# Instance normalisation over rows: giving each partition 512 consecutive rows, 8 MB from its neighbour, in place of four rows, 64 KB from its neighbour

## The chip, the cores and the metric

One core of a Trainium2 chip, with its 16 DMA engines and nothing else running. The metric is device time in microseconds (us), the median of several executions; lower is better. Executions are compared within one state (those used here are of the fast state, unless a sentence says otherwise). The kernel before has two close levels: most of its executions took 4962 to 4970 us, some 5004 to 5012. Differences of 1% are not read from a few runs here.

## The reference

```python
x = np.random.randn(256, 256, 4096).astype(np.float32)     # 65,536 rows of 16 KiB, 1.07 GB
mean = np.mean(x, axis=2, keepdims=True)
var = np.var(x, axis=2, keepdims=True)
return (x - mean) / np.sqrt(var + 1e-5)
```

Every row is normalised by itself, so it doesn't matter for the result which partition handles which row, as long as the row is written back to its place. One warning on "correct": with such an input each row already has a mean near 0 and a variance near 1, and a plain copy of x passes the comparison. The comparison shows that rows land in their places; it is weak on the arithmetic, which the change leaves alone.

## The kernel before

A tile is 128 partitions x 4 rows; 128 tiles make up the tensor. Three buffers of 64 KiB per partition take turns.

```python
x_t = x_flat.rearrange("(t p k) d -> t p k d", p=P, k=K)       # P = 128, K = 4
out_t = out_flat.rearrange("(t p k) d -> t p k d", p=P, k=K)
X = [pool.tile([P, K, d], fp32, name=f"x{s}") for s in range(BUFS)]   # BUFS = 3
```

So tile t is one contiguous piece of 8 MiB, and partition p has 64 KiB of it, right behind those of partition p - 1. One queue (SyncE's) issues all the transfers; a store and the next load alternate in it:

```python
def store(s, t):
    take(S, done[s], K)                  # the four rows are normalised
    S.dma_start(out=rows_of(out_t, t), in_=X[s][:, :, :]).then_inc(stored[s], 16)

def load(s, t, wait=True):
    if wait:
        take(S, stored[s], 16)           # the buffer's last store has landed
    S.dma_start(out=X[s][:, :, :], in_=rows_of(x_t, t)).then_inc(loaded[s], 16)

# ... first tiles cut
with S.Fori(0, rounds) as i:
    for t in range(L0, L0 + BUFS):
        store(t % BUFS, (t, BUFS, rounds, i))
        load((t + 2) % BUFS, (t + 2, BUFS, rounds, i))
# ... last tiles cut
```

VectorE sums each row and later scales three of the four; ScalarE squares and sums each row and scales the fourth. Neither is touched.

## Time and profile before

| | before |
|---|---|
| median of 2 runs | 4963.81 us |
| VectorE, ScalarE busy | 68%, 51% |
| the 16 DMA engines busy | 100% |
| bytes moved per time | 433 GB/s |
| VectorE's wait for loads | 1452.4 us, 126 times |

The DMA engines are busy for the whole span (100%), and the arithmetic waits 11.5 us in each tile for them. The lines that carry this stand in the prediction.

### The profile page before, as it was taken

What the parts mean: (1) busy time and instruction counts of PE and PEld (TensorE: products, weight loads), DVE (VectorE), ACT (ScalarE), POOL (GpSimd) and SP (SyncE); (2) the same over time, 40 slices, a digit from 0 to 9 for tenths busy, and PEclk for the clock granted to TensorE, in tenths of its full rate; (3) what the DMA queues carried; (4) which work ended last, traced back from release to release, by engine and by line L of the source; (5) the groups of instructions that cost most, each with busy time, mean ns of one, the idle gap of its engine ahead of it and who ended that gap; (6) DMA issues with size and microseconds to landing.
All of it is one profiled execution on the core that took longest, in us unless ns stands there. A gap on an engine that the chain in (4) does not pass through costs nothing.

```text
span 4960.3 us, 6348 instructions
## 1 busy us (share of the span) xinstructions
DVE 3390.1 (68%) x2439; ACT 2505.6 (51%) x1416; POOL 0.2 (0%) x4
## 2 busy tenths in 40 slices
DVE  6766666776677766777667776677666776677766
ACT  5555544555445544555445554455544555455545
POOL 0000000000000000000000000000000000000000
DMA  9999999999999999999999999999999999999999
GB/s 423 431 435 430 431 434 433 433 436 433 433 436 432 434 436 432 435 435 433 437 432 434 436 432 434 436 432 433 437 432 434 435 433 435 435 432 438 432 433 406
DMA packets 37299, 2147.52 MB, mean 433 GB/s; under 512 B 4144, under 2 KB 4144, under 8 KB 4144
## 3 DMA queue, kind: packets, MB, share of 16 engines
q1 hardware_dynamic: 37296, 2147.50, 100.0%
q14 instruction: 3, 0.02, 0.0%
HBM read 1073.74 MB, written 1073.74 MB: 433 GB/s over the span
## 4 chain that ended last, share of the span: by engine, by line
DMA 71%; DVE 19%; ACT 7%; another core or an unknown queue 1%; issue 1%; SPq 0%; ACTq 0%; DVEq 0%
DMA x<-in_x_dram 40%; DMA out_dram<-x 31%; DVE part L89 17%; ACT junk L132 3%; ACT x L140 3%; DVE nsum L91 1%; DVE x L110 1%; DVE nmean L93 1%; ACTq L182 0%; ACT std L137 0%; DVE nbias L102 0%; SPq L159 0%; SPq L154 0%; DVE rstd L100 0%
## 5 line engine op out<-in xcount | busy, mean ns | idle before, releaser
L89 DVE TENSOR_REDUCE part<-x 128x64 f32<-128x4096 f32 x512 | 2258.6, 4411 | 1452.4 <-DMA x<-in_x_dram 1452.4
L132 ACT ACTIVATE junk<-x,nmean 128x4096 f32<-128x4096 f32 x512 | 1883.0, 3678 | 2417.0 <-DVE nmean L93 2417.0
L110 DVE TENSOR_SCALAR x<-x,rstd,nbias 128x4096 f32<-128x4096 f32 x382 | 910.2, 2411 | 37.6 <-DVE nbias L102 16.4
L140 ACT ACTIVATE x<-x,nbias,rstd 128x4096 f32<-128x4096 f32 x130 | 492.2, 3786 | 0.0
L91 DVE TENSOR_REDUCE nsum<-part 128x1 f32<-128x64 f32 x512 | 112.4, 220 | 17.7
L132 ACT ACTIVATION_READ_ACCUMULATOR junk<-x,nmean 128x1 f32 x512 | 95.5, 186 | 0.0
L93 DVE TENSOR_SCALAR nmean<-nsum 128x1 f32<-128x1 f32 x512 | 78.5, 153 | 17.5
L100 DVE RECIPROCAL rstd<-std 128x1 f32<-128x1 f32 (+1 forms) x260 | 41.7, 160 | 17.2 <-ACT std L137 16.5
L102 DVE TENSOR_TENSOR nbias<-nmean,rstd 128x1 f32<-128x1 f32 (+1 forms) x260 | 41.6, 160 | 8.9
L137 ACT ACTIVATE std<-ss,eps_tile 128x1 f32<-128x1 f32 x130 | 38.3, 295 | 15.1
L124 ACT ACTIVATE std<-ss,eps_tile 128x3 f32<-128x3 f32 (+1 forms) x130 | 38.5, 296 | 4.2
L132 ACT ACT_TABLE_LOAD x1 | 1.3, 1283 | 1.2 <-DVE eps_tile L211 1.2
L124 ACT ACT_TABLE_LOAD x1 | 1.3, 1283 | 0.0
L211 DVE MEMSET eps_tile<- 128x1 f32 x1 | 0.1, 59 | 1.0 <-SPq L181 1.0
L248 POOL MEMSET const-uint8-127<- 128x1 uint8 x1 | 0.1, 102 | 0.0
L248 POOL MEMSET const-bfloat16-1.0<- 128x1 bf16 x1 | 0.1, 101 | 0.0
L248 POOL MEMSET const-float32-0.0<- 128x1 f32 x1 | 0.1, 98 | 0.2 <-issue 0.2
L248 POOL MEMSET const-float32-1.0<- 128x1 f32 x1 | 0.1, 98 | 0.0
## 6 DMA issues: line engine op xcount, KB each, us to landing
out_dram<-x SPq DMA_DIRECT2D x4, 4096.0 KB, 18.8
x<-in_x_dram SPq DMA_DIRECT2D x2, 4096.0 KB, 16.7
x<-in_x_dram SPq DMA_DIRECT2D x127, 49.2
out_dram<-x SPq DMA_DIRECT2D x126, 30.5
```

Source lines behind the costliest of these rows:

```text
L89: mine(V.tensor_reduce(out=part[s][:, r, :], in_=row, axis=AX.X, op=ALU.add))
L91: mine(V.tensor_reduce(out=nsum[s][:, c], in_=part[s][:, r, :], axis=AX.X, op=ALU.add, negate=True))
L93: V.tensor_scalar_mul(out=nmean[s][:, c], in0=nsum[s][:, c], scalar1=1.0 / d).then_inc(means, 1)
L100: mine(V.reciprocal(out=rstd[s][:, c], in_=std[s][:, c]))
L102: mine(V.tensor_mul(out=nbias[s][:, c], in0=nmean[s][:, c], in1=rstd[s][:, c]))
L110: V.tensor_scalar(out=x[:, r, :], in0=x[:, r, :], scalar1=rstd[s][:, c], scalar2=nbias[s][:, c], op0=ALU.mult, op1=ALU.add,).then_inc(dn, 1)
L124: A.activation(out=std[s][:, r0:last], in_=ss[s][:, r0:last], func=AF.Sqrt, bias=eps_tile, scale=1.0 / d).then_inc(stds, 1)
L132: A.activation(out=junk, in_=x[:, r, :], func=AF.Square, bias=nmean[s][:, c], scale=1.0, accum_out=ss[s][:, c]).then_inc(own_a, 1)
L137: A.activation(out=std[s][:, c], in_=ss[s][:, c], func=AF.Sqrt, bias=eps_tile, scale=1.0 / d).then_inc(stds, 1)
L140: A.activation(out=x[:, last - 1, :], in_=x[:, last - 1, :], func=AF.Identity, bias=nbias[s][:, c], scale=rstd[s][:, c]).then_inc(dn, 1)
L211: V.memset(eps_tile, eps).then_inc(ready, 1)
L248: nc = _bacc.Bacc("TRN2", target_bir_lowering=False, num_devices=1)
```

## The change

Its intent is to give each partition one long stretch of the tensor, 512 consecutive rows, and to walk through it four rows at a time.

```diff
-    x_t = x_flat.rearrange("(t p k) d -> t p k d", p=P, k=K)
-    out_t = out_flat.rearrange("(t p k) d -> t p k d", p=P, k=K)
+    x_t = x_flat.rearrange("(p t k) d -> t p k d", p=P, k=K)
+    out_t = out_flat.rearrange("(p t k) d -> t p k d", p=P, k=K)
```

A partition still takes 64 contiguous KiB of a tile, but the next partition's lie 512 x 16 KiB = 8 MiB further on. "Pitch" is used below for this distance from partition to partition: 64 KiB before, 8 MiB after.

## The prediction

> **What bounds the kernel now.** I read the views in this order: the page's busy shares and DMA rows, the chain of waits, the waits by engine, one tile in the timeline, and the time from issue to landing.
>
> ```profile
> DVE 3390.1 (68%) x2439; ACT 2505.6 (51%) x1416; POOL 0.2 (0%) x4
> ...
> DMA packets 37299, 2147.52 MB, mean 433 GB/s; under 512 B 4144, under 2 KB 4144, under 8 KB 4144
> ...
> q1 hardware_dynamic: 37296, 2147.50, 100.0%
> ...
> DMA 71%; DVE 19%; ACT 7%; another core or an unknown queue 1%; issue 1%; SPq 0%; ACTq 0%; DVEq 0%
> ```
>
> VectorE is busy for 68% of the span and ScalarE for 51%, but the 16 DMA engines are busy for 100% of it. The kernel reads 1073.74 MB and writes as much; 2147.5 MB at 433 GB/s take 4960 us, which is the whole span. The small packets are not data: 259 transfers with 16 semaphore writes each are the 4144 counted under 512 bytes. What remains is data in large pieces. The trace's packet records hold 32,384 packets of 65,536 bytes (one partition's four rows of 16 KiB), the rest in the halved first and last tiles. Their median duration is 2.418 us and their 95th percentile 2.419 us, so an engine moves 65,536 / 2.418 = 27.1 GB/s, and 16 of them 433.7 GB/s, whether the packet reads HBM or writes it.
>
> The chain calls 19% VectorE and 7% ScalarE, which looks as if faster arithmetic would pay. The waits say otherwise:
>
> ```profile
> DVE part L89 <- DMA x<-in_x_dram: 1452.4, 126, 12.2
> ```
>
> VectorE waits for data 126 times, 1452.4 / 126 = 11.5 us a time. One tile in the timeline:
>
> ```profile
> 2009.89 0.34 SPq L154 DMA_DIRECT2D out_dram<-x  x1
> 2010.47 0.35 SPq L159 DMA_DIRECT2D x<-in_x_dram  x1
> 2021.13 4.42 DVE L89 TENSOR_REDUCE part<-x 128x64 f32<-128x4096 f32 x1 [11.49 <-DMA x<-in_x_dram]
> ...
> 2048.46 0.34 SPq L154 DMA_DIRECT2D out_dram<-x  x1
> 2049.04 0.35 SPq L159 DMA_DIRECT2D x<-in_x_dram  x1
> 2059.77 4.42 DVE L89 TENSOR_REDUCE part<-x 128x64 f32<-128x4096 f32 x1 [11.50 <-DMA x<-in_x_dram]
> ```
>
> A tile lands at 2021.13, the next at 2059.77: the period is 38.64 us. From landing to store is 2048.46 - 2021.13 = 27.33 us of arithmetic, and 38.64 - 27.33 = 11.3 us are slack. A tile is 8.39 MB in and 8.39 MB out, which at 434 GB/s is 2 x 19.33 = 38.66 us, the period itself. In each period the one queue holds a store of tile t-1, then the load of tile t+1, so stretches of pure writing and pure reading of some 19 us alternate.
>
> ```profile
> x<-in_x_dram SPq DMA_DIRECT2D x127, 49.2
> out_dram<-x SPq DMA_DIRECT2D x126, 30.5
> ```
>
> These fit the same picture: a store is issued with 11.3 us of the earlier load still ahead and takes 19.3, in all 30.6 (seen: 30.5); the load behind it takes 19.3 more, 49.9 (seen: 49.2).
>
> [...]
>
> [...] The kernel before, with a pitch of 64 KiB, moves 433 / 2 = 217 GB/s per direction[...]. It can't show the slow case.
>
> [...]
>
> **The change part by part.**
>
> 1. Instructions. The order on VectorE, ScalarE, SyncE and the rest is the same as before, row for row (190, 91 and 50 rows). Each partition still takes four adjacent rows of a tile, 65,536 contiguous bytes, so I expect the same 37,296 packets of the same sizes, nothing removed and nothing added. The arithmetic keeps its 27.33 us a tile. Load and store use the same mapping, so each row returns to its place and the result is right.
>
> 2. Addresses. The start of partition p moves from p x 65,536 bytes to p x 512 x 16,384 = p x 8,388,608 bytes: exactly 8 MiB, a power of two, plus 65,536 times the tile's number. In one transfer all 128 packets agree in their address modulo 8 MiB; all that tells the 16 streams apart there is how far each has come in its 64 KiB.
>
> 3. What that costs. [...] A transfer of 8.39 MB takes 40.2 us instead of 19.33, and the period becomes 80.4 us.
>
> 4. What of it is hidden: nothing. The DMA queue already sets the period and its slack is zero. The slack is on the arithmetic's side, 11.3 us a tile, and grows to 80.4 - 27.3 = 53.1.
>
> 5. Sum. 128 x (80.4 - 38.66) = 5,343 us more than 4,964, or 10,307 us. [...] I take 10,300. The ends, where arithmetic isn't overlapped, are some 20 us in either kernel and change nothing.
>
> **The rivals.**
>
> A. It costs little or nothing (about 4,960 us). For it: the order of instructions and the packets stay the same[...]. The packet records show starts scattered over the 2.4 us of a packet, not in step: some 0.15 us apart, which is about 4 KiB of progress. [...]
>
> B. A part of it, say a factor of 1.2 to 1.8 (6,000 to 9,000 us). For it: with 64 KiB in a run the streams of one transfer cover a four times wider window of addresses[...], and the load and the store in flight lie two tiles, 128 KiB, apart in two tensors. If what they share is coarse[...], a wider window means more places to spread over. I can't size it from anything in the profile before.
>
> C. Worse[...] (up to 20,000 us). [...] Here the queue alternates: for 19 us only reads, then only writes. [...] Against it: when engines drift apart at the limit, some will be on the store while others are on the load[...].
>
> D. A new wait takes over. With three buffers, a load of t+2 needs the store of t-1 to have landed, and that store is two places ahead of it on the same queue. As the transfers slow down, every tile of arithmetic has more time, so no engine becomes the bound; I rule this out.
>
> E. It gets faster. [...] One in a hundred.
>
> **The range and the chances.** [...] half of my weight is on a factor of 1.8 to 2.3, or 8,900 to 11,400 us. B has a quarter, A a tenth, C and other ways of being worse 15%. The middle of these is [...] 10,300 us. The range that cuts about a tenth at each side is 6,000 to 13,000 us; it gives up A at one side and the full form of C at the other. Slower by over 2%: 0.90; within 2%: 0.09; faster: 0.01.
>
> **What would show it.** If it is right, the profile after has 37,296 packets again, DMA engines busy all the time, and a mean near 208 GB/s in each of the 40 slices; packets of 64 KiB at about 5.0 us and widely scattered instead of all at 2.418; every group of VectorE and ScalarE with its old mean (4411, 3678, 2411 ns); VectorE's wait for data at 53.1 us a tile, 6,700 us in all; and a store landing 53.1 + 40.2 = 93 us after its issue, a load 133 us. Step 1 is wrong if the number or sizes of packets change, for then the change is one of descriptors and not of addresses. Step 3 is wrong in size if packets take 3 to 4 us (B) or near 10 us (C), and wrong altogether if they keep 2.4 (A). If reads and writes differ, for instance writes slow and reads not, then [...] my single factor is a mean of them. Step 4 is wrong if the period exceeds the packets' time, with the DMA engines idle.

## More of the kernel before

One more view is wanted for later, the rate in 40 equal slices of the span; it is level from the second slice to the last but one:

```profile
GB/s 423 431 435 430 431 434 433 433 436 433 433 436 432 434 436 432 435 435 433 437 432 434 436 432 434 436 432 433 437 432 434 435 433 435 435 432 438 432 433 406
```

## The result, and the profile after

The changed kernel took 7134.01 us (two runs, 7132.27 and 7135.74), with a ratio of 1.437 to the kernel before (95% interval 1.431 to 1.443). Ratios here are the mean time of one kernel's fast runs over that of the other's fast runs in the same rounds, so not quite the ratio of the medians that are quoted. It is slower, as forecast, and inside the range of 6,000 to 13,000 us, but the forecast was 10,300: the kernel lost 2170 us where 5,336 were predicted. The size was wrong.

The page of the changed kernel, with the engines' busy time, the rate by slices, the packets, the shares of the chain, two of the costliest groups, and the times from issue to landing:

```profile
DVE 3390.6 (48%) x2439; ACT 2505.6 (35%) x1416; POOL 0.2 (0%) x4
...
GB/s 247 260 275 305 304 306 305 310 296 302 309 309 305 302 301 297 304 306 313 302 301 301 312 310 302 297 305 310 297 299 286 308 304 308 303 303 309 309 299 317
DMA packets 37299, 2147.52 MB, mean 301 GB/s; under 512 B 4144, under 2 KB 4144, under 8 KB 4144
...
q1 hardware_dynamic: 37296, 2147.50, 97.9%
...
another core or an unknown queue 52%; DVE 45%; issue 2%; ACT 0%; DMA 0%; DVEq 0%; ACTq 0%; SPq 0%
...
L89 DVE TENSOR_REDUCE part<-x 128x64 f32<-128x4096 f32 x512 | 2258.7, 4412 | 3612.3 <-DMA x<-in_x_dram 3612.3
...
L110 DVE TENSOR_SCALAR x<-x,rstd,nbias 128x4096 f32<-128x4096 f32 x382 | 910.3, 2411 | 37.7 <-DVE nbias L102 17.1
...
x<-in_x_dram SPq DMA_DIRECT2D x127, 81.0
out_dram<-x SPq DMA_DIRECT2D x126, 54.3
```

The number of packets is the same to the last one, and so are the engines' busy times (3390.6 us against 3390.1) and the mean of each instruction. All that differs is how long the DMA engines need: 301 GB/s in place of 433, still 97.9% busy. The chain of waits is a trap here: where it said DMA before it says "another core or an unknown queue" for 52%. The kernel has one core, and the view of waits and the timeline name the same stretches, ahead of VectorE's first sum in a tile, as a wait for the load:

```profile
DVE part L89 <- DMA x<-in_x_dram: 3612.3, 127, 44.0
```

```profile
3018.97 4.42 DVE L89 TENSOR_REDUCE part<-x 128x64 f32<-128x4096 f32 x1 [26.56 <-DMA x<-in_x_dram]
...
3046.40 0.34 SPq L154 DMA_DIRECT2D out_dram<-x  x1
3046.98 0.35 SPq L159 DMA_DIRECT2D x<-in_x_dram  x1
3072.74 4.42 DVE L89 TENSOR_REDUCE part<-x 128x64 f32<-128x4096 f32 x1 [26.61 <-DMA x<-in_x_dram]
```

From landing to store is 3046.40 - 3018.97 = 27.43 us, the same arithmetic as before; this tile's period is 53.77 us in place of 38.64, and VectorE waits 26.6 us in it in place of 11.5. Over all tiles the wait is 3612.3 / 127 = 28.4 us. The wait grew by 3612.3 - 1452.4 = 2159.9 us and the span by 7133.6 - 4960.3 = 2173.3: nearly the whole loss is in the wait for transfers.

The trace's packet records say in what form. Duration in ns of the packets of 65,536 bytes, 32,384 in each kernel:

```
kernel    mean   10%   25%   50%   75%   90%   99%   within 1% of the fastest
before    2420  2418  2418  2418  2418  2418  2432   99%
after     3403  2418  2831  3209  3779  4451  6441   13%
```

Packets were nearly all alike, at 2418 ns (99% within 1%); now one in eight (13%) still takes no longer and the rest are held up by different amounts. The mean grew by 3403 / 2420 = 1.406, and the engines are busy 97.9% and not 100%; 1.406 / 0.979 = 1.436 is the measured ratio to within 0.1%.

The trace holds one more thing, which bears on all that follows: the times of the 16 semaphore writes that end each transfer, taken here as one from each engine. In the changed kernel the first and the last engine finished 1.7 us apart in the first of the 40 slices (median of its transfers), 3.6 in the second, 18.4 in the third and 37.6 in the fourth, and some 30 from then on, as long as a whole transfer takes. The rate in these four slices is 247, 260, 275 and 305 GB/s. So the engines start in step and drift apart, and the rate rises as they do. That is a coincidence in time; no run set the drift by itself.

### The profile page after: what moved, and what is told of

Read it like the earlier page. It is cut to its first block, busy times and chain, and to the rows that moved or that the text cites.

```text
span 7133.6 us, 6348 instructions
## 1 busy us (share of the span) xinstructions
DVE 3390.6 (48%) x2439; ACT 2505.6 (35%) x1416; POOL 0.2 (0%) x4
## 3 DMA queue, kind: packets, MB, share of 16 engines
q1 hardware_dynamic: 37296, 2147.50, 97.9%
HBM read 1073.74 MB, written 1073.74 MB: 301 GB/s over the span
## 4 chain that ended last, share of the span: by engine, by line
another core or an unknown queue 52%; DVE 45%; issue 2%; ACT 0%; DMA 0%; DVEq 0%; ACTq 0%; SPq 0%
DVE part L89 31%; DVE x L110 10%; DVE nsum L91 2%; DVE nmean L93 1%; DVE nbias L102 1%; DVE rstd L100 0%; DMA x<-in_x_dram 0%; ACT junk L132 0%; DVEq L68 0%; ACTq L182 0%; DVEq L105 0%; DVEq L214 0%; ACT std L137 0%; ACT L124 0%
## 5 line engine op out<-in xcount | busy, mean ns | idle before, releaser
L89 DVE TENSOR_REDUCE part<-x 128x64 f32<-128x4096 f32 x512 | 2258.7, 4412 | 3612.3 <-DMA x<-in_x_dram 3612.3
## 6 DMA issues: line engine op xcount, KB each, us to landing
out_dram<-x SPq DMA_DIRECT2D x126, 54.3
```

The source lines that it names most:

```text
L89: mine(V.tensor_reduce(out=part[s][:, r, :], in_=row, axis=AX.X, op=ALU.add))
```

## The experiments

Eighteen kernels ran. The questions were: is it the equality of the addresses or the distance; does it hit reads, writes or both; why is the loss 44% and not the 108% that the prediction put on a tile's period (80.4 us in place of 38.66, the author's estimate, which nothing in the profile before showed); and what do copies without the arithmetic lose. The theory for the third, called W, is this: what counts is how wide a window of addresses modulo a large power of two the streams in flight cover. In the changed kernel the 128 packets of a transfer all cover the same 64 KiB modulo 8 MiB. The main rivals are that each start of a packet at a far address has its cost (P), and that reads and writes at once make the difference.

**One direction alone.** First only the loads, then only the stores, use the new mapping. Rows then land in wrong places.

```diff
# first run: before, with
+    x_t = x_flat.rearrange("(p t k) d -> t p k d", p=P, k=K)
# second run: before, with
+    out_t = out_flat.rearrange("(p t k) d -> t p k d", p=P, k=K)
```

> Only the loads use the 8 MiB mapping; the stores keep 64 KiB, so rows land in the wrong place and the result is wrong on purpose. The change cost 7134 - 4964 = 2170 us in both directions. Theory 1 (each direction pays for itself, alike): about half, 4964 + 1085 = 6050 us, with half of the large packets still at 2.418 us. Theory 2 (reads and writes at far addresses get in each other's way): less than a third of it, under 5690 us. Theory 3 (only reads are hurt): near 7130 us.

> Only the stores use the 8 MiB mapping; wrong result on purpose. Theory 1: about 6050 us, and together with the run that moves only the loads the two extra times add up to 2170 us. Theory 2: both extras together clearly under 2170 us. Theory 3 (only reads are hurt): 4964 us here; if only writes are hurt, near 7130 us.

Measured: loads alone 5707.13 us (ratio 1.143), stores alone 6092.67 us (1.220). Against 4964 us these are 743 and 1129 us, together 1872 of the 2170, and far stores cost half as much again as far loads. (The kernel before ran at both of its levels in these rounds; by the ratios, 0.143 and 0.220 of 0.437 leave 0.074, some 370 us, in place of the 298.) The page of each, the rate by slices, the loads' run first:

```profile
GB/s 314 341 350 359 360 367 373 376 380 380 380 380 383 385 381 380 386 389 377 381 387 384 379 380 385 387 379 383 389 381 381 380 390 384 380 384 385 385 377 377
```

```profile
GB/s 318 300 319 343 359 363 349 355 360 362 353 355 356 359 355 349 362 354 364 351 355 358 363 351 355 353 365 354 359 356 360 355 352 359 358 357 351 360 354 342
```

In the first, 66% of the large packets stayed within 1% of the fastest, which would fit half of them being stores at the old addresses. In the second only 37% did, although half are loads at the old addresses: at least a quarter of these loads were held up too, so a far direction also slows the near one, and the 743 and 1129 us are costs to the kernel, not to one direction's own packets. Theory 1 gives the larger part of the loss, with unequal halves; theory 3 falls; of theory 2 there remain the 298 us or so that appear only when both directions are far, and the kernel with reversed stores, below, takes that up.

**Distance or equality.** The same far packets, with a pitch of 511 rows in place of 512.

```diff
-    x_t = x_flat.rearrange("(p t k) d -> t p k d", p=P, k=K)
+    x_t = bass.AP(x_flat.tensor, 0, [[4*d, ntiles], [511*d, P], [d, K], [1, d]])   # out_t alike
```

> The mapping of the change, but with 511 rows in place of 512 from partition to partition: 8 MiB less 16 KiB. Packets are as far apart as before and as long; some rows are done twice and the last 128 not at all, so the result is wrong on purpose. If distance itself costs[...], 7130 us as with 512. If the equality of the addresses modulo a large power of two costs, the time returns to 4964 us within 2%. Something between would say that 16 KiB steps undo only some of the collisions.

Measured: 4990.65 us, ratio 1.0006. All of the loss is gone (interval 0.993 to 1.008), with packets that lie 8 MiB less 16 KiB apart. The page has the rate of the kernel before:

```profile
GB/s 422 433 435 431 435 433 433 436 432 436 434 433 437 432 434 436 432 437 433 433 437 432 435 435 432 437 433 433 436 433 436 434 433 436 433 433 436 432 430 398
```

Being 8 MiB less 16 KiB apart costs nothing here (1.0006); lying at equal addresses modulo 8 MiB does (1.437). What in the memory such addresses share, no trace here shows.

**Shorter runs.** The changed kernel with each transfer cut into four, then into two, and the first cut on the kernel before as a control.

```diff
-        S.dma_start(out=rows_of(out_t, t), in_=X[s][:, :, :]).then_inc(stored[s], 16)
+        for j in range(4):                                     # or 2
+            q = slice(j * K // 4, (j + 1) * K // 4)
+            S.dma_start(out=rows_of(out_t, t)[:, q, :], in_=X[s][:, q, :]).then_inc(stored[s], 16)
# loads alike; the waits for a whole tile go from 16 to 16 * 4
```

> The changed kernel, with each load and store of 64 KiB per partition cut into four transfers of 16 KiB per partition[...], one after the other in the queue. Theory W (a run of 64 KiB lets the streams spread[...]): near [...] 10300 us, packets of 16 KiB at about 1.26 us in place of 0.6. Rival (length of the run does not matter[...]): about 7130 us plus what more packets cost, at most a few per cent.

> Control: the kernel before (64 KiB between partitions) with the same cut into four transfers of 16 KiB per partition. If the 9325 us of the cut far kernel came from the more numerous packets and semaphores, much of it shows here (say over 5500 us). If it came from the addresses, this is 4964 us within 2%.

> The changed kernel with each transfer cut in two, 32 KiB per partition. Whatever the cause of the difference between 64 KiB (ratio 1.437) and 16 KiB (1.868), this should lie between: about 1.6, 7950 us. If it is at either end, there is a step between two sizes and not a slope.

Measured: cut in four 9325.17 us (ratio 1.868), in two 7698.96 us (1.549), the control 5035.49 us (1.012). The first lies between the two times expected, nearer to W's. The control matters: at near addresses four times the packets and semaphores cost 1%, so the rest of the 1.868 is put down to the addresses, 1.868 / 1.012 = 1.85; a cost of each transfer that arises at far addresses alone is not excluded. A shorter run makes it worse, in a slope and not a step (1.437 with 64 KiB, 1.549 with 32, 1.868 with 16). The packets and rates of the cut far kernel and of its control, in this order:

```profile
DMA packets 146596, 2147.58 MB, mean 230 GB/s; under 512 B 16288, under 2 KB 16288, under 8 KB 16288
```

```profile
DMA packets 146597, 2147.58 MB, mean 427 GB/s; under 512 B 16289, under 2 KB 16289, under 8 KB 16289
```

**Packet or window.** The cut changes two things at once: packets become 16 KiB, and the streams of a transfer cover only 16 KiB. This kernel changes only the first. A gap of 64 bytes after each row of the tile on the chip keeps rows from being joined into one packet, while a partition's four rows still follow one another.

```diff
-    X = [pool.tile([P, K, d], fp32, name=f"x{s}") for s in range(BUFS)]
+    X = [pool.tile([P, K, d + 16], fp32, name=f"x{s}")[:, :, :d] for s in range(BUFS)]
```

> The changed kernel with 64 bytes of unused space after each row of 16 KiB in the tiles on the chip: a packet can then hold only one row, 16 KiB, [...] the streams of a transfer still cover 64 KiB. Theory W (what counts is how wide a window of addresses modulo 8 MiB the streams in flight cover): as the changed kernel, about 7130 us, although packets are 16 KiB. Rival P (each start of a packet at a far address costs): as the cut kernel, about 9300 us. Check: packets of 16,384 bytes, 129,000 of them.

Measured: 7099.18 us, ratio 1.428; the trace has 131,072 packets of 16,384 bytes. The page of this kernel:

```profile
DMA packets 135219, 2147.52 MB, mean 303 GB/s; under 512 B 4144, under 2 KB 4144, under 8 KB 4144
```

Packets of 16 KiB cost nothing more here (1.428 against 1.437) as long as the window stays at 64 KiB. P falls, and W stands so far.

**A wider window.** The pitch is 8 MiB less 1 KiB, then 8 MiB less 256 bytes, which slides the partitions against one another by so much each.

```diff
+    x_t = bass.AP(x_flat.tensor, 0, [[4*d, ntiles], [512*d - 256, P], [d, K], [1, d]])   # 1 KiB; 64 for 256 bytes
```

> The mapping of the change with 8 MiB less 1 KiB from partition to partition (16 KiB less gave the full rate). Wrong result on purpose. Over 128 partitions the shifts add up to 127 KiB, so the window of addresses modulo 8 MiB of one transfer grows from 64 to 191 KiB. Theory W: most of the loss goes, under 5500 us. If shifts must reach about a packet's length between neighbours to help, it stays near 7130 us.

> The mapping of the change with 8 MiB less 256 bytes from partition to partition; wrong result on purpose. The window of one transfer grows from 64 KiB to 64 + 127 x 0.25 = 96 KiB. Theory W, read off the windows measured so far (32 KiB 1.55, 64 KiB 1.44, 191 KiB 1.03): between the last two, 1.2 to 1.35, 5950 to 6700 us. If[...] a small shift does nothing: 1.44, 7130 us.

Measured: 5123.28 us (1.029) and 6116.90 us (1.231), both where W had put them. All windows together (the run's length plus 127 shifts):

```
window of one transfer modulo 8 MiB    ratio to before
16 KiB   (cut in four)                 1.868 (1.85 with the cut's own cost taken off)
32 KiB   (cut in two)                  1.549
64 KiB   (the change)                  1.437
96 KiB   (8 MiB less 256 bytes)        1.231
191 KiB  (8 MiB less 1 KiB)            1.029
2096 KiB (511 rows)                    1.001
```

**Other pitches.** 2 MiB and 512 KiB. Tiles then overlap in rows and most rows are left out, so far fewer different bytes are touched.

```diff
+    x_t = bass.AP(x_flat.tensor, 0, [[4*d, ntiles], [128*d, P], [d, K], [1, d]])   # 2 MiB; 32*d for 512 KiB
```

> As the change, with 128 rows (2 MiB) from partition to partition; tiles overlap in rows and most rows are left out, so the result is wrong on purpose. [...] 12% at 2 MiB: 5570 us. If equality modulo 2 MiB is as bad as modulo 8 MiB: 7130 us. If only higher address bits matter with runs of 64 KiB: 4964 us.

> As the change, with 32 rows (512 KiB) from partition to partition; wrong result on purpose. [...] 1.3% here: 4964 to 5030 us. If any large power of two does the harm, some of the 7130 us should be seen.

Measured: 5558.91 us (1.120) and 4974.00 us (1.002). The expectation of 5570 us for the first is within 0.3%; for the second, 1.3% of loss were expected and 0.2% found. With a pitch of 2 MiB the packets of a transfer have four different addresses modulo 8 MiB, with 512 KiB sixteen: the second loses next to nothing (0.2%). The first doesn't fit W as it stands: four windows of 64 KiB cover 256 KiB modulo 8 MiB and cost 12%, while one window of 191 KiB cost 2.9%. So the bytes covered don't settle the cost alone; how finely the partitions are shifted against one another may count as well, and no run here separates the two.

**Reads and writes meeting.** The changed kernel, with the stores walking through the tiles in the other direction.

```diff
+    out_t = bass.AP(out_flat.tensor, 508*d, [[-4*d, ntiles], [512*d, P], [d, K], [1, d]])
```

> As the change, but the result of tile t goes where that of tile 127 - t belongs (wrong on purpose): the distance between the window being read and the one being written, 128 KiB in the changed kernel throughout, now runs from about +8 MiB through zero to about -8 MiB in one execution. The loads alone cost 14% and the stores alone 22%, 36% in all, but both cost 44%. If the missing 8% are reads and writes meeting in the same places, the rate moves along the 40 slices, with stretches better than the changed kernel's 305 GB/s; the best possible by the sum is 433 / 1.36 = 318 GB/s. If not, it stays at 305 in all slices, and the time at 7130 us. Also: the changed kernel starts at 247 GB/s and rises to 305 within three slices. If that is because of the tile numbers read and written first, the start changes here; if because the engines start in step, it stays.

Measured: 7074.58 us, ratio 1.426. Its page:

```profile
GB/s 248 268 293 308 306 311 308 310 300 300 306 301 307 306 304 302 299 298 306 305 302 309 311 309 306 307 307 309 308 310 296 306 312 308 310 303 308 310 306 318
```

No stretch is clearly better than in the changed kernel, whatever the distance between the two windows. The theory that the surplus of 298 us comes from reads and writes meeting in the same places falls, and that surplus stays open; some 60 us of it are that the engines idle 2.1% of the span when both directions are far (151 us), against 0.7 and 0.8% with one (42 and 46 us). The slow start is there again though the stores begin at the other end, and so is the drift: the first and the last engine finish a transfer 1.8, 5.4, 42.5 and 33.0 us apart in the first four slices. That speaks for the engines starting in step as the cause of the slow start; since the loads begin where they did, it is not shown.

**Copies without the arithmetic.** Why even the run of 16 KiB, at 1.85, lost less than the prediction's 108% was still open, so the last six kernels leave out the arithmetic. Three copy from tensor to tensor, with nothing on the chip between:

```python
S.dma_start(out=out_t[t][:, q, :], in_=x_t[t][:, q, :]).then_inc(sem, 16)    # 12 in flight (3 of 64 KiB)
```

> No arithmetic: tiles of 128 partitions x 16 KiB copied from the input tensor straight to the output tensor, 12 copies in flight, 64 KiB between partitions; wrong result on purpose (a copy). [...] 5020 us.

> The same copies with 8 MiB between partitions[...]. [...] 10425 us[...]; then HBM on both sides accounts for the rest of the difference. If the cut kernel's factor of 1.85 shows here too, about 9280 us[...].

> The copies at 8 MiB with 64 KiB per partition in one transfer, 3 in flight (as many bytes). Theory W: the wider window softens it here too, to about 1.44 to 1.6 times the near copy, 7200 to 8000 us. If HBM on both sides keeps the factor [...] whatever the run: 10400 us.

Measured: 3247.31 us for the near copy, 12391.61 us for the far one of 16 KiB (the mean of its two fast runs; the third, 12563.32, was slow), 11373.69 us for the far one of 64 KiB. All three expectations missed. The near copy isn't held at the rate of the kernel before: it moves 1073.74 MB / 3247.31 us = 331 GB/s per direction, where that kernel has 433 / 2 = 217. At the far addresses a longer run helps hardly at all (a factor of 1.09 between the two), so W as it stands is a finding about traffic between HBM and a tile, not about any traffic. Two things differ here besides the missing tile. In the far copy of 64 KiB the engines stay in step: the first and the last finish a transfer 5.2 us apart, of the 88 us between transfers. And in that of 16 KiB the engines were busy only 77% of the span, so the packets' time doesn't explain all of it. One line from the page of each, near 16 KiB, far 16 KiB, far 64 KiB:

```profile
HBM read 1073.74 MB, written 1073.74 MB: 662 GB/s over the span
```

```profile
HBM read 1073.74 MB, written 1073.74 MB: 174 GB/s over the span
```

```profile
HBM read 1073.74 MB, written 1073.74 MB: 190 GB/s over the span
```

The other three copy through a tile, loads from one queue and stores from a second, so that both run at once:

```python
# queue 1: wait until the slot's store has landed, then
nc.sync.dma_start(out=X[s][:, :, :], in_=x_t[t][:, q, :]).then_inc(loaded[s], 16)
# queue 2: wait until the slot's load has landed, then
nc.scalar.dma_start(out=out_t[t][:, q, :], in_=X[s][:, :, :]).then_inc(stored[s], 16)
```

> No arithmetic: 16 KiB per partition loaded into a tile on the chip from one queue and stored again from a second queue as soon as it has landed, 12 tiles in turn, 64 KiB between partitions; a copy on purpose. Bound by the 16 engines as the kernel before: [...] 4950 to 5050 us[...].

> The same at 8 MiB. [...] 10425 us, and the difference to the cut kernel (9325 us) is that loads and stores run at once. If loads and stores at once don't matter: about 9300 us.

> The same at 8 MiB with 64 KiB per partition in one transfer, 3 tiles. Theory W for any traffic between tensor and tile: about the changed kernel's 7130 us, at most 7500. If loads and stores at once take the softening away, as in the straight copy: over 9000 us.

Measured: near 5001.89 us (1073.74 MB / 5001.89 us = 215 GB/s per direction), far with 16 KiB 8169.01 us (131 GB/s), far with 64 KiB 6777.25 us (158 GB/s); both far times are means of two fast runs, and the third of each, 8310.91 and 6935.58, was slow. The first met its expectation, the second neither of its two, the third W's. The profiled run of the last was the slow one, so its profile isn't read here. Over the whole execution the 64 KiB run again loses less. But the page of the 16 KiB run, its rate by slices and its two queues, q1 the loads and q10 the stores, says that this is a mean over a changing rate:

```profile
GB/s 183 189 195 199 198 200 205 216 227 234 245 242 249 258 266 259 256 257 265 270 267 270 272 296 300 302 295 320 320 326 309 317 316 308 295 301 309 295 302 247
...
q1 hardware_dynamic: 73728, 1073.77, 65.2%
q10 hardware_dynamic: 73728, 1073.77, 34.3%
```

It starts at 183 GB/s and climbs to some 310, near the 64 KiB run's mean of 2 x 158. So most of the advantage of the longer run lies in the first half, and W holds in this setting only with that limit. The first seven slices have 92 to 103 GB/s per direction, about the 104 that the prediction had for the changed kernel (208 / 2); as a mean over an execution that was met in no setting with 16 KiB: 115 in the cut kernel (230 / 2), 131 here, 87 in the straight copy. Why the settings differ stays open. The two queues also turn the order of the first experiment round: as many load packets as store packets took nearly twice the engines' time (65.2% against 34.3%).

## Why the prediction was wrong

**Steps 1 and 2 (instructions, packets, addresses)** were right to the packet: 37,296 again, of the same sizes, and no instruction's mean moved by more than 1 ns. The kernel at 511 rows (1.0006 against 1.437) shows that the equality of the addresses is the cause, as step 2 had it, and not their distance.

**Step 3 (what that costs)** is the step that failed, in the size of one term: "A transfer of 8.39 MB takes 40.2 us instead of 19.33, and the period becomes 80.4 us". That is 108% more for every transfer, the author's estimate; nothing in the profile before showed it. That equal addresses would cost was right; the factor was mis-sized. A packet took 3.40 us in the mean, a factor of 1.406, and with 2.1% of idle time 1.436. That is what the prediction's own sign for rival B had, "packets take 3 to 4 us". The estimate took no account of the length of the run, and the runs show that the loss depends on it: the same traffic with windows of 16, 32 and 64 KiB has 1.87, 1.55 and 1.44, the control for the cut 1.01, and the gap between rows (1.428) shows that it is not the packet's length but the stretch of addresses that a transfer covers (W, with the limits said above). Of the kernels with the arithmetic only that with runs of 16 KiB comes near the estimate, with 85% (1.85); what lies between the two is not explained. The single factor also took the engines to be in one condition throughout; the rate of 247 GB/s in the first slice, with the engines in step, and of some 305 later shows that they weren't.

**Step 4 (nothing hidden)** was right but for the 2.1% in which the engines idled. With the measured period of 7133.6 / 128 = 55.7 us the step's own arithmetic gives a wait of 55.7 - 27.3 = 28.4 us a tile, which is what VectorE waited, and, with half a period of 27.9 us for a transfer, a store landing after 28.4 + 27.9 = 56.3 us and a load after 84.2; seen were 54.3 and 81.0.

**Step 5 (the sum)** multiplied the wrong factor by the right number of tiles.

**Rivals.** B was the outcome, with its cause: it said that "with 64 KiB in a run the streams of one transfer cover a four times wider window of addresses" (the runs have 1.44 with 64 KiB against 1.87 with 16), put it at 6,000 to 9,000 us, and had a quarter of the weight; nothing in the profile before could size it, as the prediction said. It could have been sized beforehand only by a run like the cut ones. A, C and E fall by the time: 7134 us is neither near 4,960 nor under it, and not above the forecast's 10,300. In A, the starts "some 0.15 us apart" were read as the distance between engines; the landings of the kernel before say that they finish a transfer 6.7 us apart, nearly three packets, so that reading was too small. D was ruled out a little too firmly. The queue's own waits in the changed kernel have

```profile
SPq L68 <- DMA out_dram<-x: 216.4, 50, 53.5
```

where the kernel before had 44.9 us in 3 waits: in 50 tiles the load did wait for an earlier store to land. Since a load and a store were still ahead in the queue, the DMA engines remained 97.9% busy, so this is not the bound, but it may be where some of the 2.1% went.

## What to carry to other kernels

When a DMA-bound kernel is re-tiled, compare the distance from partition to partition in HBM, and not only the size of the packets: at a large power of two (2 and 8 MiB here; 512 KiB cost 0.2%) the kernel took 12 and 44% longer with the same packets, and what the profile shows of it is a lower rate (386 and 301 GB/s in place of 433) and, at 8 MiB, packet times that scatter (2418 ns at the 10th percentile, 4451 at the 90th). Breaking the equality by 1 KiB a partition gave back nearly all of it (1.029), and 16 KiB all (1.0006); a longer contiguous run per partition softened it in this kernel, though hardly in a straight copy (a factor of 1.09 between the two). And the factor here belonged to its shape (1.87, 1.55 and 1.44 by the run): before one is used, ask which of the sizes in its setting the cause depends on. Look at the rate by slices too: here the mean of 301 GB/s hides a start at 247.
